# The beginning of a two-layer decoder trunk: loads in order of use, first products 512 columns wide, parameter loads later

## The chip, the core and the metric

The kernel runs on one core of one Trainium2 chip. The metric is the time of one execution in microseconds (us). The engines are called as in the profile: PE (TensorE), DVE (VectorE), ACT (ScalarE), POOL (GpSimd) and SP (SyncE, which here only starts DMAs). Each works through its own instructions in order and waits on semaphores for the others.

## What is computed

A trunk of two layers on x of 256 tokens by 1024 features, all float32. Each layer is a half-weighted SwiGLU block, a token mixer (gated linear attention, "gla", in layer 0; gated DeltaNet, "gdn", in layer 1) and a second SwiGLU block, each with an RMSNorm ahead and a residual sum behind, and a last RMSNorm.

```python
for i in range(DEPTH):                                   # DEPTH = 2
    x = x + 0.5 * swiglu(rmsnorm(x, norm_w[i, 0]), ffn_w_in[i, 0], ffn_w_out[i, 0])
    h = rmsnorm(x, norm_w[i, 1])
    x = x + (gla_mixer(h, ...) if i == 0 else gdn_mixer(h, ...))
    x = x + 0.5 * swiglu(rmsnorm(x, norm_w[i, 2]), ffn_w_in[i, 1], ffn_w_out[i, 1])
return rmsnorm(x, final_norm_w)

def swiglu(h, w_in, w_out):                              # w_in 1024 x 5632, w_out 2816 x 1024
    g, u = jnp.split(h @ w_in, 2, axis=-1)
    return (jax.nn.silu(g) * u) @ w_out
```

## The kernel before, in words

The stages are f00, gla, f01, f10, gdn, f11 (f: a SwiGLU block, class `FeedForward`). The 256 tokens are two blocks t = 0 and 1 of 128; x is transposed by PE to `xT` (`turn_x`, L307: four transposes of 128 by 128 for block t and feature half g, then four scaled copies to `xT`'s high part by ACT, and `lower`, four DVE operations that give the low part). Every product runs as three matmuls of a reduced float32 form: high by high, high by low and low by high.

**Weights.** Class `Weights` (L28) loads each weight block as a raw tile by SP (`_load`, four tiles in rotation) and cuts it into *parts* of 128 by 1024 numbers. A part is made in two steps: `high` has ACT cast the raw numbers (L69, "hi"), and `low` has DVE subtract the cast from the raw numbers (L76, "lo"). `take` hands the next part to PE. `high(n, held)` casts up to n further parts, but only while the number cast so far is below `taken - held + LOOK`, with LOOK = 7. In the stages' hand-ordered stretches `low` and `high` stand at fixed places between PE's work, so a part's cast and subtraction happen at the place where the count reaches it. In the `run` of a `FeedForward` stage `advance` refills to seven ahead after each take, and the instructions are ordered by a planner; everywhere else the order is as written.

**The start of a stage.** `step_over` (L1385) ends one stage and begins the next. It begins the next stage's first products (`units(0)`: block t = 0; `second_half` then ends them and runs `units(1)`: block 1), and calls `high(2, 4)` when a quarter has been issued twice:

```python
        low()
        high(2, 4)          # L1410, L1411
        second_half(st, fill)
```

For gla and gdn the first products are those of `first_columns` (L382), 512 columns wide; it takes all four parts at its first step (`parts.extend(W.take() for _ in range(4))`, L388). For a `FeedForward` they are those of `part` (L434), gate and up columns apart, 256 columns wide, and a part is taken when it is reached: two of four parts at the place of `high(2, 4)`.

**Behind it.** In gla's `run` (L704) the second value columns (`token_columns`, parts 5 to 8 of the stage) are followed by key and query columns (`load`: part 9 first). In gdn's `run` twelve pairs of `load` parts follow; `step(i)` (L1229) issues PE's products of pair i, parts 5 + 2i and 6 + 2i of the stage, in the pieces `fill(n[0])` to `fill(n[3])`; `fill(n[0])` is followed on DVE by the evacuation of pair i - 1 and two `low` calls, later in the step come the convolution's operations on DVE and two calls of `high(2)`, together two casts.

**The beginning of the program.** SP loads x in three pieces with the first two raw tiles between them (L213 to L217), POOL loads six small parameter tensors at once (`load_parameters`), PE warms up with `busy` products on constants, `turn_x` for block 0 and both halves comes first, then the first product part, then `turn_x` for block 1 between the parts. `parameters` (an Exp, a PE transpose, an ACT copy) stands in the middle of it.

Of the kernel before, what the change touches and what calls it, by code (L numbers as in the profile page):

```python
# [11 lines left out]
AF = mybir.ActivationFunctionType  # L12
# [15 lines left out]
class Weights:  # L28
# [79 lines left out]
def trunk(ctx: ExitStack, tc: tile.TileContext, x_in, norm_w, ffn_w_in, ffn_w_out, gla_w_in, gla_w_gk, gla_b_gk,  # L108
# [198 lines left out]
    def turn_x(N, t, g):  # L307
# [7 lines left out]
        for k in range(4):  # L315
            nc.scalar.activation(his[k], ps[:, k, :], AF.Copy, scale=ws[k])
# [65 lines left out]
    def first_columns(N, name, pss):  # L382

        parts = []

        def units(t):
            if t == 0:
                parts.extend(W.take() for _ in range(4))  # L388
            pss[t] = gup(f"tm_{name}{t}")[:, 0, :]
            for s in range(4):  # L390
                for k in range(2):
                    xh, xl = (N.xT[:, 2 * s + k, u + t * P:u + (t + 1) * P] for u in (0, 256))
                    hi, lo = parts[s]
                    nc.tensor.matmul(pss[t], lhsT=xh, rhs=hi[:, k, :], start=(s + k == 0), stop=False)
                    nc.tensor.matmul(pss[t], lhsT=xh, rhs=lo[:, k, :], start=False, stop=False)
                    nc.tensor.matmul(pss[t], lhsT=xl, rhs=hi[:, k, :], start=False, stop=(s == 3 and k == 1))
                    yield
                if t == 1:
                    low()
                    high(1, 3 - s)  # L400

        return units
# [25 lines left out]
    class FeedForward:  # L428
        factor, quarter, mids = 0.5, 4, {}

        def __init__(self, N):
            self.N, self.parts, self.ps, self.am, self.aTs = N, [], {}, [], {}

        def part(self, t, s, c):  # L434

            N, i = self.N, 2 * s + c
            while len(self.parts) <= i:
                self.parts.append(W.take())
            if t not in self.ps:
                self.ps[t] = gup(f"g0_{N.name}{t}")  # L440
            hi, lo = self.parts[i]
            for k in range(4):
                o = self.ps[t][:, c, 0:256]
                xh, xl = (N.xT[:, 4 * s + k, u + t * P:u + (t + 1) * P] for u in (0, 256))
                nc.tensor.matmul(o, lhsT=xh, rhs=hi[:, k, :], start=(s + k == 0), stop=False)  # L445
                nc.tensor.matmul(o, lhsT=xh, rhs=lo[:, k, :], start=False, stop=False)  # L446
                nc.tensor.matmul(o, lhsT=xl, rhs=hi[:, k, :], start=False, stop=(s == 1 and k == 3))  # L447
                yield

        def units(self, t):  # L450
            for s in range(2):
                for c in range(2):
                    yield from self.part(t, s, c)
                    if t == 1:
                        low()
                        high(1, 3 - 2 * s - c)

        def first(self, t):
            N, ps = self.N, self.ps[t]
            sl = small(f"sl0_{N.name}{t}", 256, tag="t1")  # L460
            nc.scalar.activation(sl, ps[:, 0, 0:256], AF.Silu, scale=N.r[t][:, 0:1])
            a = small(f"a0_{N.name}{t}", 256, tag="t1")
            nc.vector.scalar_tensor_tensor(a, ps[:, 1, 0:256], N.r[t][:, 0:1], sl, op0=ALU.mult, op1=ALU.mult)
# [131 lines left out]
    def gla(N):  # L595
# [22 lines left out]
        def gates():  # L618
            rows_bc(N)
            hold["z"] = narrow(N, "z")  # L620

# [4 lines left out]
        st.units = first_columns(N, "v0", ps0)  # L626
# [205 lines left out]
    def gdn(N):  # L832
# [63 lines left out]
        st.units = first_columns(N, "dr0", ps0)  # L896
# [562 lines left out]
    load_parameters()  # L1459
    N, st = make(stages[0])  # L1460
    with manual():
        constants()
        for g in range(2):
            lower = turn_x(N, 0, g)
# [3 lines left out]
        busy(8)  # L1468
        if isinstance(st, FeedForward):
            part = lambda *a: [None for _ in st.part(*a)]  # L1470
            part(0, 0, 0)
            for g in range(2):
                turn_x(N, 1, g)()
                high(1)
                low()
            part(0, 0, 1)
            parameters()
            rms(N, 0)
            for c in range(2):
                part(1, 0, c)  # L1480
            rms(N, 1)
            high(1)
            low()
            for t in range(2):
                for c in range(2):
                    part(t, 1, c)
# [3 lines left out]
        else:  # L1490
            turn_x(N, 1, 0)()
            turn_x(N, 1, 1)()
# [3 lines left out]
            parameters()  # L1496
# [43 lines left out]
```

## Time and profile before

| | us |
|---|---|
| three runs, median (lowest, highest) | 1045.27 (1044.95, 1045.68) |
| the profiled execution | 1045.1 |
| its span, first to last instruction | 1043.4 |
| PE busy in the span | 1027.3 |
| DVE busy | 701.0 |
| ACT busy | 590.4 |

The rows of the trace are in a section below. A row of the timeline gives the start, the busy time, the engine, the line, the operation, the output and the inputs, their sizes, how many instructions are merged in it and, in brackets, how long the engine sat idle before it and what ended that. Consecutive matmuls overlap, so the pace of PE is read from start to start, not from the busy time of one. A few records of PE can be missing from a trace or be given to a neighbouring line.

### The profile page before, as it was taken

Reading aid. Unit: us, or ns where it says so; the run is one execution under the profiler, and the core shown is the slowest. Engines: PE = TensorE matmul, PEld = TensorE weight load, DVE = VectorE, ACT = ScalarE, POOL = GpSimd, SP = SyncE. Lnnn points to the kernel's source line nnn. Section 1 sums busy time; section 2 is a strip of 40 time slices with the busy share of each in tenths; the row PEclk is TensorE's granted clock in tenths of the full one; section 3 lists DMA queues with packets and bytes.
Section 4 is the critical chain, followed back from the end, with each engine's and each line's share of the span. In section 5 each row is a group of like instructions: output and inputs, shape, how many; then the busy total and the mean of one; then the engine's idle time right before and its main releaser. Section 6 shows DMA issues by size and latency. Waiting matters only on the chain.

```text
span 1043.4 us, 15585 instructions
## 1 busy us (share of the span) xinstructions
PE 1027.3 (98%) x6162; PEld 892.0 (85%) x6162; DVE 701.0 (67%) x956; ACT 590.4 (57%) x1019; POOL 212.6 (20%) x250
## 2 busy tenths in 40 slices
PE   8999999999999999999999999999999999999996
PEld 8888888789889888888988888879989898888885
DVE  5866666666577666666766666578998776666664
ACT  7655555573556555555655555478677565555552
POOL 2111111103201111110111111117734401111111
PEclk9999999999999999999999999999999999999999
DMA  8764645444364564744564655544443156556431
GB/s 295 242 235 139 231 158 172 155 130 158 141 222 162 202 212 152 240 139 148 210 233 155 209 175 188 164 125 135 144 135 131 47 198 240 191 173 216 147 122 41
DMA packets 132410, 180.26 MB, mean 173 GB/s; under 512 B 5212, under 2 KB 111760, under 8 KB 132336
## 3 DMA queue, kind: packets, MB, share of 16 engines
q1 hardware_dynamic: 131712, 178.14, 51.0%
q0 software_dynamic: 416, 0.84, 0.4%
q8 instruction: 48, 0.79, 0.3%
q10 hardware_dynamic: 208, 0.29, 0.1%
q14 instruction: 26, 0.21, 0.1%
HBM read 178.20 MB, written 1.05 MB: 172 GB/s over the span
## 4 chain that ended last, share of the span: by engine, by line
PE 91%; DVE 3%; POOL 2%; issue 1%; DMA 1%; ACT 1%; SPq 0%; POOLq 0%; DVEq 0%; ACTq 0%
PE ps_f L341 29%; PE ps_f L342 15%; PE acc_f L414 7%; PE acc_f L413 7%; PE acc_f L415 7%; PE ps_d L576 2%; PE g_f L445 1%; PE g_f L447 1%; PE g_f L446 1%; PE ps_d L578 1%; PE ps_d L577 1%; DMA x<-in_x_dram 1%; POOL Mc L1002 1%; DVE lo L76 1%; PE acc_gdn L415 1%
## 5 line engine op out<-in xcount | busy, mean ns | idle before, releaser
L76 DVE TENSOR_TENSOR lo<-raw,hi 128x1024 fp32r<-128x1024 f32 x336 | 431.4, 1297 | 198.8 <-ACT hi L69 198.7
L69 ACT CAST hi<-raw 128x1024 fp32r<-128x1024 f32 x338 | 348.1, 1046 | 190.6 <-PE acc_f L415 83.7
L341 PE MATMUL ps_f<-xT_f,hi 128*128 128x512 f32 x1280 | 455.6, 398 | 0.0
L342 PE MATMUL ps_f<-xT_f,lo 128*128 128x256 f32 x1280 | 359.1, 281 | 0.0
L341 PEld LDWEIGHTS ps_f<-xT_f,hi 128*128 128x128 f32 x1280 | 240.5, 188 | 58.4
L342 PEld LDWEIGHTS ps_f<-xT_f,lo 128*128 128x128 f32 x1280 | 241.7, 189 | 2.8
L371 POOL TENSOR_TENSOR pair_f<-plo_f,Rb_f 128x512 f32<-128x512 f32 x76 | 102.8, 1352 | 558.6 <-DVE plo_f L369 558.6
L413 PE MATMUL acc_f<-hi,aT_f 128*128 128x512 f32 x352 | 138.4, 393 | 0.0
L414 PE MATMUL acc_f<-lo,aT_f 128*128 128x512 f32 x352 | 137.9, 392 | 0.0
L415 PE MATMUL acc_f<-hi,aT_f 128*128 128x512 f32 x352 | 137.0, 389 | 0.0
L413 PEld LDWEIGHTS acc_f<-hi,aT_f 128*128 128x128 f32 x352 | 66.1, 188 | 15.1
L415 PEld LDWEIGHTS acc_f<-hi,aT_f 128*128 128x128 f32 x352 | 66.1, 188 | 14.4
L414 PEld LDWEIGHTS acc_f<-lo,aT_f 128*128 128x128 f32 x352 | 66.1, 188 | 10.7
L405 ACT CAST aT_f<-a_f 128x256 fp32r<-128x256 f32 x80 | 32.5, 407 | 71.6 <-DVE a_f L483 71.4
L481 ACT ACTIVATE sl_f<-pair_f 128x256 f32<-128x256 f32 x80 | 33.5, 418 | 54.6 <-POOL pair_f L371 48.6
L369 DVE TENSOR_TENSOR plo_f<-ps_f,plo_f 128x512 f32<-128x512 f32 x80 | 54.7, 683 | 12.6 <-ACT plo_f L368 12.5
L406 DVE TENSOR_TENSOR aT_f<-a_f,aT_f 128x256 fp32r<-128x256 f32 x80 | 34.0, 425 | 36.0 <-ACT aT_f L405 36.0
L576 PE MATMUL ps_d<-xT_gdn,hi 128*128 128x256 f32 x192 | 56.5, 294 | 0.1
L578 PE MATMUL ps_d<-xT_gdn,lo 128*128 128x256 f32 x192 | 54.4, 283 | 1.1 <-DVE lo L76 1.1
L577 PE MATMUL ps_d<-xT_gdn,hi 128*128 128x256 f32 x192 | 54.2, 282 | 0.0
L368 ACT COPY plo_f<-ps_f 128x512 f32<-128x512 f32 x80 | 46.4, 580 | 12.8 <-PE ps_f L342 12.8
L483 DVE TENSOR_TENSOR a_f<-sl_f,pair_f 128x256 f32<-128x256 f32 x80 | 33.0, 413 | 10.4 <-ACT sl_f L481 10.4
(363 smaller groups left out, 1299.0 us busy)
## 6 DMA issues: line engine op xcount, KB each, us to landing
raw<-in_ffn_w_in_dram SPq DMA_DIRECT2D x80, 1024.0 KB, 5.4
raw<-in_ffn_w_out_dram SPq DMA_DIRECT2D x44, 1024.0 KB, 5.4
raw<-in_gdn_w_in_dram SPq DMA_DIRECT2D x16, 1024.0 KB, 5.4
raw<-in_gla_w_in_dram SPq DMA_DIRECT2D x12, 1024.0 KB, 5.1
raw<-in_ffn_w_in_dram SPq DMA_DIRECT2D x16, 512.0 KB, 3.5
raw<-in_gla_w_out_dram SPq DMA_DIRECT2D x4, 1024.0 KB, 5.0
raw<-in_gdn_w_out_dram SPq DMA_DIRECT2D x4, 1024.0 KB, 5.0
out_dram<-fin SPq DMA_DIRECT2D x3, 256.0 KB, 2.1
```

The costliest lines, as they stand in the source:

```text
L69: nc.scalar.copy(hv, src)
L76: self.nc.vector.tensor_tensor(lv, src, hv.bitcast(F32), op=ALU.subtract)
L341: nc.tensor.matmul(ps, lhsT=hi[:, k, :], rhs=N.xT[:, k, :], start=(k == 0), stop=False)
L342: nc.tensor.matmul(ps[:, 0:256], lhsT=lo[:, k, :], rhs=N.xT[:, k, 0:256], start=False, stop=(k == KT - 1))
L369: nc.vector.tensor_tensor(t, ps[:, :, 0:256], t, op=ALU.add)
L371: (eng or nc.gpsimd).tensor_tensor(dst, t, N.Rb.unsqueeze(1).broadcast_to([P, 2, 256]), op=ALU.mult)
L413: nc.tensor.matmul(accs[t][n], lhsT=ah, rhs=hi[:, 0, c], start=first, stop=False)
L414: nc.tensor.matmul(accs[t][n], lhsT=ah, rhs=lo[:, 0, c], start=False, stop=False)
L415: nc.tensor.matmul(accs[t][n], lhsT=al, rhs=hi[:, 0, c], start=False, stop=last)
L576: nc.tensor.matmul(o, lhsT=hi[:, k, :], rhs=xh, start=(k == 0), stop=False)
L577: nc.tensor.matmul(o, lhsT=hi[:, k, :], rhs=xl, start=False, stop=False)
L578: nc.tensor.matmul(o, lhsT=lo[:, k, :], rhs=xh, start=False, stop=(k == KT - 1))
```

## The change

What it does, piece by piece:

- Each `FeedForward`'s first weights come as four raw tiles of 256 rows with gate and up columns side by side (512 wide), each loaded by two DMAs of 256 KB, where there were four tiles of 512 rows with 256 columns and one DMA of 512 KB each.
- `FeedForward` uses `first_columns` for its first products: 24 matmuls of 512 columns for a block of tokens, in place of 48 of 256. Both blocks write one two-bank PSUM tile.
- `first_columns` takes a part when it reaches it, for all stages; its generator yields after three matmuls, twice a part.
- At the program's start SP issues x block 0 first half, raw tile 0, x block 1 first half, raw tile 1, then x's other halves, raw tiles 2 and 3. PE's order is: transposes of block 0 half 0, `busy`, products of block 0 with part 0, transposes of block 1 half 0, products of block 1 with part 0, transposes of the other halves, products with parts 1, 2 and 3 for both blocks. The first four scaled copies go to DVE. A one-element Silu stands on ACT ahead of the first cast.
- `load_parameters` moves behind the second block's norm, `parameters` into gla's `gates`.

```diff
@@ Weights._load
-            self.nc.sync.dma_start(tv, src)
+            if len(src.shape) == 3:
+                self.nc.sync.dma_start(tv, src)
+            else:
+                for a in range(shape[0]):
+                    self.nc.sync.dma_start(tv[:, a, :].rearrange("p (c f) -> p c f", c=src.shape[2]), src[:, a])
@@ trunk
-            for i in range(2):
-                for c in (0, FF):
-                    sub_rows(blk(w1, i * 512, 512, c, 256), 0, 4, 256)
+            for i in range(4):
+                w4 = w1[i * 256:(i + 1) * 256, :].rearrange("(k p) (c f) -> p k c f", p=P, c=2)
+                sub_rows(W.add_raw(w4[:, :, :, 0:256], (2, 512)), 0, 2, 512)
...
-    nc.sync.dma_start(x[:, 0, 512:1024], xv[:, 0, 512:1024])
+    W._load(0)
+    nc.sync.dma_start(x[:, 1, 0:512], xv[:, 1, 0:512])
     W._load(1)
-    nc.sync.dma_start(x[:, 1, :], xv[:, 1, :])
+    for t in range(2):
+        nc.sync.dma_start(x[:, t, 512:1024], xv[:, t, 512:1024])
+    W._load(3)
@@ turn_x(N, t, g, on_vector=False)
+            if on_vector:
+                nc.vector.tensor_scalar_mul(his[k], ps[:, k, :], ws[k])
+            else:
+                nc.scalar.activation(his[k], ps[:, k, :], AF.Copy, scale=ws[k])
@@ first_columns
+        def part(t, s):
+            while len(parts) <= s:
+                parts.append(W.take())
+            if not pss:
+                both = gup(f"tm_{name}")
+                pss.update({0: both[:, 0, :], 1: both[:, 1, :]})
+            hi, lo = parts[s]
+            for i, (u, w, k) in enumerate((u, w, k) for u, w in ((0, hi), (256, hi), (0, lo)) for k in range(2)):
+                nc.tensor.matmul(pss[t], lhsT=N.xT[:, 2 * s + k, u + t * P:u + (t + 1) * P], rhs=w[:, k, :],
+                                 start=(s + i == 0), stop=(s == 3 and i == 5))
+                if i % 3 == 2:
+                    yield
         def units(t):
-            if t == 0:
-                parts.extend(W.take() for _ in range(4))
-            pss[t] = gup(f"tm_{name}{t}")[:, 0, :]
             for s in range(4):
-                for k in range(2):
-                    ...
+                yield from part(t, s)
                 if t == 1:
                     low()
                     high(1, 3 - s)
@@ FeedForward
-        factor, quarter, mids = 0.5, 4, {}
+        factor, quarter, mids = 0.5, 2, {}
+            self.part, self.units = first_columns(N, f"g0_{N.name}", self.pss)
@@ gla: gates
             hold["z"] = narrow(N, "z")
+            parameters()
@@ the start
-    load_parameters()
     N, st = make(stages[0])
...
+            nc.scalar.activation(small("silu", 1), half, AF.Silu)
+            lower = turn_x(N, 0, 0, True)
             high(1)
             lower()
             low()
+            busy(8)
+            part(0, 0)
+            lower = turn_x(N, 1, 0)
+            high(1)
+            lower()
+            low()
+            part(1, 0)
+            lowers = [turn_x(N, t, 1) for t in range(2)]
+            high(1)
+            for lower in lowers:
+                lower()
+            for t in range(2):
+                part(t, 1)
+            low()
             rms(N, 0)
             high(1)
             low()
             for t in range(2):
+                part(t, 2)
+            rms(N, 1)
+            load_parameters()
+            for t in range(2):
+                part(t, 3)
                 st.first(t)
                 high(1)
                 low()
```

## Rows read from the trace of the kernel before

**Rows 1.** The page: its span, and the busy time and share of each engine.
```profile
span 1043.4 us, 15585 instructions
...
PE 1027.3 (98%) x6162; PEld 892.0 (85%) x6162; DVE 701.0 (67%) x956; ACT 590.4 (57%) x1019; POOL 212.6 (20%) x250
```
**Rows 2.** Waits of PE over the whole span: who waited for whom, us in total, times, the longest.
```profile
PE ps_d L578 <- DVE lo L76: 1.1, 2, 0.6
PE g_f L445 <- ACT hi L69: 1.0, 1, 1.0
```
**Rows 3.** The timeline of the first 24 us.
```profile
1.53 2.50 PE L236 MATMUL busy<-ones,ident 128*128 128x128 f32 x10 [1.53 <-POOL ident masks.py:199]
...
4.24 1.89 PE L312 MATMUL xps_f<-ident,x 128*128 128x128 f32 x8
...
5.45 1.14 ACT L316 ACTIVATE xT_f<-xps_f,nwc 128x128 fp32r<-128x128 f32 x4 [0.91 <-PE xps_f L312]
...
7.85 1.04 ACT L69 CAST hi<-raw 128x1024 fp32r<-128x1024 f32 x1 [1.25 <-DMA raw<-in_ffn_w_in_dram]
...
8.93 1.22 DVE L76 TENSOR_TENSOR lo<-raw,hi 128x1024 fp32r<-128x1024 f32 x1 [1.17 <-ACT hi L69]
...
12.04 1.10 PE L312 MATMUL xps_f<-ident,x 128*128 128x128 f32 x8 [0.27 <-DMA x<-in_x_dram]
12.74 1.14 ACT L316 ACTIVATE xT_f<-xps_f,nwc 128x128 fp32r<-128x128 f32 x4 [1.86 <-PE xps_f L312]
...
13.91 1.12 DVE L320 SCALAR_TENSOR_TENSOR xT_f<-xps_f,nwc,xT_f 128x128 fp32r<-128x128 f32 x4 [1.60 <-ACT xT_f L316]
...
20.51 1.28 ACT L461 ACT_TABLE_LOAD   x1
21.81 0.47 ACT L461 ACTIVATE sl_f<-g_f,rstd_f 128x256 f32<-128x256 f32 x1
...
23.59 0.28 PE L342 MATMUL ps_f<-xT_f,lo 128*128 128x256 f32 x1
```
**Rows 4.** DMA at the start: two lines of the issues of the first 30 us (out, in, queue, count, KB each, median us from issue to landing), and two stretches of 1 us (busy us and instructions of PE, PE's weight loads, DVE, ACT and POOL, granted clock, DMA share, GB/s).
```profile
raw<-in_ffn_w_in_dram SPq DMA_DIRECT2D x4, 512.0 KB, 8.7
...
x<-in_x_dram SPq DMA_DIRECT2D x1, 512.0 KB, 9.3
...
9.00:10.00 1.00, 0.33 (x1) 0.13 (x1) 1.00 (x1) 1.00 (x5) 0.00 (x0) 1.00 1.06 166
...
12.00:13.00 1.00, 0.96 (x9) 0.96 (x10) 0.32 (x1) 0.26 (x1) 0.00 (x0) 1.00 1.09 383
```
**Rows 5.** The pace of PE, from the timeline of PE: the first and the last of 36 matmuls of 256 columns in f00, and of 22 starts of 512 columns in gla.
```profile
18.83 0.28 PE L445 MATMUL g_f<-hi,xT_f 128*128 128x256 f32 x1
...
23.03 0.28 PE L447 MATMUL g_f<-hi,xT_f 128*128 128x256 f32 x1
...
207.96 0.40 PE L394 MATMUL tm_v<-hi,xT_gla 128*128 128x512 f32 x1
...
212.73 0.39 PE L589 MATMUL tm_v<-hi,xT_gla 128*128 128x512 f32 x1
```
**Rows 6.** The timeline of ACT in three step-overs, the casts at the place of `high(2, 4)`: into gla (the first of the two is a narrow part of 128 by 128), into f10 and into gdn (narrow first again).
```profile
202.74 1.26 ACT L69 CAST hi<-raw 128x128 fp32r<-128x128 f32 x2
...
500.51 1.07 ACT L69 CAST hi<-raw 128x1024 fp32r<-128x1024 f32 x1
...
687.43 1.26 ACT L69 CAST hi<-raw 128x128 fp32r<-128x128 f32 x2
```
**Rows 7.** gla: ACT's casts behind the gates' copies, DVE's subtractions, and the first product on PE that reads the low half of part 9, in order of time.
```profile
208.48 3.89 ACT L69 CAST hi<-raw 128x1024 fp32r<-128x1024 f32 x4
...
220.75 1.21 DVE L76 TENSOR_TENSOR lo<-raw,hi 128x1024 fp32r<-128x1024 f32 x1
...
226.00 0.28 PE L578 MATMUL ps_gk<-xT_gla,lo 128*128 128x256 f32 x1
...
227.46 2.35 DVE L76 TENSOR_TENSOR lo<-raw,hi 128x1024 fp32r<-128x1024 f32 x2
```
**Rows 8.** gdn, steps 6, 7 and 9: the first product of PE that reads the low half of a pair's second part (746.49 in step 6, 765.86 in step 9), DVE's two subtractions in the step, and PE's waits in between.
```profile
746.49 0.28 PE L578 MATMUL ps_d<-xT_gdn,lo 128*128 128x256 f32 x1
...
749.23 2.41 DVE L76 TENSOR_TENSOR lo<-raw,hi 128x1024 fp32r<-128x1024 f32 x2
...
750.51 0.38 PE L578 MATMUL ps_d<-xT_gdn,lo 128*128 128x256 f32 x1 [0.65 <-DVE lo L76]
...
765.86 0.28 PE L578 MATMUL ps_d<-xT_gdn,lo 128*128 128x256 f32 x1
...
770.10 2.03 PE L1048 MATMUL Y<-Mc,U 64*64 64x32 f32 x62 [0.78 <-ACT U L1036]
...
771.75 2.35 DVE L76 TENSOR_TENSOR lo<-raw,hi 128x1024 fp32r<-128x1024 f32 x2
...
773.01 0.39 PE L578 MATMUL ps_d<-xT_gdn,lo 128*128 128x256 f32 x1 [0.45 <-DVE lo L76]
```
**Rows 9.** The end of the program: PE's last matmul, and two stretches behind it (columns as in rows 4; the granted clock is the number ahead of the last two).
```profile
1034.51 0.39 PE L415 MATMUL acc_f<-hi,aT_f 128*128 128x512 f32 x1
...
1038.00:1040.00 2.00, 0.00 (x0) 0.00 (x0) 1.01 (x2) 0.72 (x1) 0.92 (x1) 1.00 0.14 54
1040.00:1042.00 2.00, 0.00 (x0) 0.00 (x0) 0.00 (x0) 0.00 (x0) 0.00 (x0) 0.54 0.68 262
```

More of the change, by code (lines that the diff above doesn't have):

```diff
@@ L305, in enter, with turn_x @@
         return N
-    def turn_x(N, t, g):
+    def turn_x(N, t, g, on_vector=False):
         ps = acc4(f"xps_{N.name}{t}{g}")
@@ L315, in turn_x @@
         for k in range(4):
-            nc.scalar.activation(his[k], ps[:, k, :], AF.Copy, scale=ws[k])
+            if on_vector:
+                nc.vector.tensor_scalar_mul(his[k], ps[:, k, :], ws[k])
+            else:
+                nc.scalar.activation(his[k], ps[:, k, :], AF.Copy, scale=ws[k])
         def lower():
@@ L384, in first_columns @@
         parts = []
+        def part(t, s):
[10 more added lines that the diff above has]
+                    yield
         def units(t):
-            if t == 0:
-                parts.extend(W.take() for _ in range(4))
-            pss[t] = gup(f"tm_{name}{t}")[:, 0, :]
             for s in range(4):
-                for k in range(2):
[L392 to L397, printed above, removed]
+                yield from part(t, s)
                 if t == 1:
@@ L400, in units @@
                     high(1, 3 - s)
-        return units
+        return part, units
     def split(dst_hi, dst_lo, src):
@@ L428, in trunk @@
     class FeedForward:
-        factor, quarter, mids = 0.5, 4, {}
+        factor, quarter, mids = 0.5, 2, {}
         def __init__(self, N):
[L432 to L456, printed above, removed]
+            self.N, self.pss, self.am, self.aTs = N, {}, [], {}
+            self.part, self.units = first_columns(N, f"g0_{N.name}", self.pss)
         def first(self, t):
-            N, ps = self.N, self.ps[t]
+            N, ps = self.N, self.pss[t]
             sl = small(f"sl0_{N.name}{t}", 256, tag="t1")
-            nc.scalar.activation(sl, ps[:, 0, 0:256], AF.Silu, scale=N.r[t][:, 0:1])
+            nc.scalar.activation(sl, ps[:, 0:256], AF.Silu, scale=N.r[t][:, 0:1])
             a = small(f"a0_{N.name}{t}", 256, tag="t1")
-            nc.vector.scalar_tensor_tensor(a, ps[:, 1, 0:256], N.r[t][:, 0:1], sl, op0=ALU.mult, op1=ALU.mult)
+            nc.vector.scalar_tensor_tensor(a, ps[:, 256:512], N.r[t][:, 0:1], sl, op0=ALU.mult, op1=ALU.mult)
             self.am.append(a)
@@ L625, in gla @@
         ps0 = {}
-        st.units = first_columns(N, "v0", ps0)
+        _, st.units = first_columns(N, "v0", ps0)
         st.first = lambda t: v_evac(ps0[t], t, 0)
@@ L895, in gdn @@
         ps0, ev0 = {}, gate_evac(N, srn, 0, 4, nwb[:, 256:384])
-        st.units = first_columns(N, "dr0", ps0)
+        _, st.units = first_columns(N, "dr0", ps0)
         st.first = lambda t: hold.update({"finish": ev0(ps0[t], t, t == 1)})
@@ L1462, in trunk @@
         constants()
-        for g in range(2):
-            lower = turn_x(N, 0, g)
+        if isinstance(st, FeedForward):
+            part = lambda *a: [None for _ in st.part(*a)]
+            nc.scalar.activation(small("silu", 1), half, AF.Silu)
+            lower = turn_x(N, 0, 0, True)
             high(1)
@@ L1467, in trunk @@
             low()
[L1468 to L1477, printed above, removed]
+            busy(8)
[12 more added lines that the diff above has]
+            low()
             rms(N, 0)
-            for c in range(2):
-                part(1, 0, c)
-            rms(N, 1)
             high(1)
@@ L1484, in trunk @@
             for t in range(2):
-                for c in range(2):
-                    part(t, 1, c)
+                part(t, 2)
[3 more added lines that the diff above has]
+                part(t, 3)
                 st.first(t)
@@ L1490, in trunk @@
         else:
-            turn_x(N, 1, 0)()
-            turn_x(N, 1, 1)()
+            for t in range(2):
+                for g in range(2):
+                    turn_x(N, t, g)()
             rms(N, 0)
@@ L1495, in trunk @@
             W.prefill()
-            parameters()
+            load_parameters()
             fill = filler(st.units(0))
```

## The prediction

> **What bounds the kernel now.** I read the page first: PE is busy 1027.3 of 1043.4 us [rows 1], so time is won or lost only where PE starts earlier, does less, or is made to wait. The waits of PE come next: they are few, and the largest behind the start is for low halves of weights in gdn, 1.1 us in two waits [rows 2]. Weights are ready only just in time there; a reader should keep that. Then I read the timeline of the start, where PE's stream becomes dense only at 12.04, when the last piece of x lands [rows 3], and the places in gla and gdn where the change alters the order in which weights are made ready [rows 6 to 8]. The sum is made against the profiled execution, 1045.1 us for a span of 1043.4; it lies 0.2 below the median of 1045.27.
>
> **Part 1, width of the products.** 256 columns go at (23.03 - 18.83) / 35 = 0.120 us, 512 columns at (212.73 - 207.96) / 21 = 0.227 [rows 5]. A FeedForward stage has 96 of the one before and 48 of the other after: 11.52 against 10.90, 0.6 us less. In f01, f10 and f11 these products are dense, so the 0.6 counts in full; transposes between them cost the same either way. Three stages: -1.7 (I take 0.57 each, since starts right behind transposes are a little slower). f00's share is in part 2.
>
> **Part 2, the start.** Loads: before, the 512 KB tiles took 8.7 us to land (median) and x's second block 9.3 [rows 4], part of it beside POOL's parameter loads, when the rate fell to 166 GB/s against 383 two us later [rows 4]. Raw tile 0 had landed at 7.85, when its cast started [rows 3]; it is now second in the queue, without those loads. I bound it by 5.4 and 7.8 and take 6.0, an estimate: 768 KB at some 300 GB/s, the middle of these rates, behind a first 2 us, plus one for the slowest engine. Extra DMA issues stand on SP only, which waits for buffers anyway.
>
> Now the chain, with durations from [rows 3]. Four transposes start at 4.24 and end at 5.4, as before. DVE makes the four high copies (not shown on DVE; bounds 0.8 and 1.4 around L320's 1.1, the nearest row, which I take) and the four low ones (1.1): 7.55. ACT loads Silu's table behind the copy of the norm weights (1.28) and runs the small Silu: 6.0, then the cast: 7.05. Low half of part 0: 7.55 + 1.2 = 8.7. PE, in order, cannot pass the two products that read it (0.5): 9.2. The next transposes stand behind them: 9.7. ACT's four copies: 10.85; DVE starts low copies only when all four are done, as at 12.74 and 13.91. Two low copies and the four products left: 12.3. The eight transposes, whose first four feed ACT after 0.6; eight copies on ACT: 15.1; the last four low copies behind them on DVE: 16.25; low half of part 2: 17.4. From there PE is dense: 14 products, 3.2, with their tail 20.8. But then Silu of block 0 (0.47) stands ahead of the cast of part 4 (1.04), and that ahead of its low half (1.22): 23.6. The first product of the main loop that reads it ran at 23.59 before. So PE is through with its first products near 22.2, some 0.9 earlier than before, and waits the gain away: **0.0**, with -0.8 (quick copies on DVE, half the coupling) and +1.5 (raw tile 0 at 7.8, which goes through the chain almost one to one) as ends. The moved parameter loads cost nothing: POOL issues them behind the second norm, and its next work was idle-waiting; the weights they run beside are needed some 12 us later.
>
> **Part 3, what the lazy take does to the look-ahead.** This is the term that decides. At `high(2, 4)` the stage's parts 0 to 3 have been cast. gla and gdn had taken four parts there, so the limit was 4 - 4 + 7 = 7 and two casts went out; f10 had taken two, limit 5, one cast. The rows show just this: two, one, two [rows 6]. After the change `first_columns` has taken two at that place, since a quarter of two yields, issued twice, is two parts. So gla and gdn cast one, and each later part takes the place of its successor, until some call meets its limit. In gla that is the first `high(2, 2)`, behind `k_evac(0, pk[0])`, in gdn the end of step 12. In the steps of gdn the old count sits at the limit exactly, so nothing catches up.
>
> Price in gla: part 9's low half moves from DVE's place at 220.75 to that at 227.46, behind the scan and the difference there, and is ready at 227.46 + 1.2 = 228.7. PE reads it at 226.00 [rows 7]. PE waits **2.7**; it has nothing else queued, and it is dense behind, so nothing gives that back. Bounds 1.5 and 3.5.
>
> Price in gdn: in each step the second part's low half now comes from the first `low` of the same step instead of the step before. In steps 1 to 5 it still arrives within 0.1 us of its product. In step 6 DVE is late with the solve's gathering: 749.23 + 1.2 = 750.45, read at 746.49 [rows 8]: 4.0. PE's old wait up to 750.51, 0.7 with the pace taken off, goes: net 3.3. DVE meanwhile works on things already ready, so its places don't shift. In step 9 the low half is ready at 771.75 + 1.2 = 772.95, behind the solve's back substitution; PE would read it at 765.86 + 3.3 = 769.2: 3.8. The waits of 0.78 and 0.45 behind it [rows 8], some 1.8 with weight loads and a short one that follows, fall away: net 2.0. Sum **5.3**, bounds 3 (DVE drawn earlier by what PE no longer contends for) and 9 (its places shift with PE by half).
>
> **Part 4, `parameters` in gla.** The transpose moves and costs the same. On ACT, Exp behind Silu needs a table load that wasn't there: L461's took 1.28 and the activation started 1.30 after it [rows 3]. Queued behind it are the casts from 208.48 [rows 7]: 208.5 + 1.3 + two short ones 0.4 + 1.05 = 211.2, low half 212.5; token columns read it 0.23 behind 212.73 [rows 5]. Zero, with 0.4 to spare; +0.1 for small things. The Trainium skill, "ScalarE: Activation LUTs", section "What ACT_TABLE_LOAD costs", gives about 2.66 us for a switch, a drain included, and so speaks against moving an Exp between Silu and Ln. The row shows half of that; by the page PE would wait, which is rival 4.
>
> **Sum.** -1.7 + 0.0 + 2.7 + 5.3 + 0.1 = +6.4: 1045.1 + 6.4 = 1051.5.
>
> **The rivals.**
> 1. Look-ahead costs nothing (the other side). If more than one cast goes out at `high(2, 4)` in gla, or the low halves reach DVE before its long operations, the 8.0 vanish: 1045.1 - 1.7 + 0.1 = 1043.5. Against it: [rows 6] show the count obeyed, and [rows 2] that there was no slack. It decides at whether part 9's low half ends before 226.0.
> 2. The clock falls in the new waits. The trace shows ten busy matmuls in 2.50 us at the start and eight transposes in 1.89 [rows 3], half the later pace, 1.2 against 2.4 GHz, from 1.53 to 6.13. If each of the two waits of about 4 us in gdn were followed by such a stretch of 4.6 us at half pace, each would cost 2.3 more: 1056.1. Against it: after the last matmul at 1034.51 the granted clock was still 1.00 in 1038 to 1040 and fell behind 1040 [rows 9]. The Trainium skill, "TensorE: Matmul & The Clock Gate", section "HAM oscillation", warns that a matmul stream broken by waits is throttled again; this trace has a wait of that length without it.
> 3. The start slips: raw tile 0 no sooner than 7.8: +1.5, 1053.0. For it: four loads share the queue from the first. Against it: x and POOL's loads leave its way.
> 4. The table load of part 4 with its drain holds ACT longer than its row: with a drain as long as the load itself, 1.3 more, less the 0.4 to spare, PE waits 0.9 for the token columns: 1052.4. (That is the page's rule of part 4; by its figure the wait is 1.0.) Against it: the activation began 1.30 behind the load's start [rows 3].
> 5. DVE's places shift in full with PE's waits, so that later second parts wait too. If the seven steps from 6 to 12 each paid half of what steps 6 and 9 pay on average (5.3 / 2), that is 9 more: 1060.5. Against it: DVE is without idle in that stretch.
>
> **How the numbers follow.** Forecast 0.60, rival 1 0.13, rival 2 0.07, rival 3 0.10, rival 4 0.05, rival 5 0.05. The range 1047.5 to 1056.5 holds the forecast with its bounds and rivals 2 to 4, and leaves out rivals 1 and 5 and a little of the forecast's tails, 0.2. This kernel's measurement can tell 0.2% (2.1 us) from no change: faster is below 1043.2, slower above 1047.4. Rival 1 lies on the edge of faster: 0.05 faster, 0.13 same with a good startup added to a cheap look-ahead, 0.82 slower.
>
> **What would show it.** Right: one cast between the last copy of x and the first evacuation in gla and gdn; a wait of PE for a low half of 2.7 near gla's first key product, of about 4 in gdn's steps 6 and 9; the first column products ending earlier but the main loop of f00 starting at the same time, behind a wait for a low half of about 1 us; 512-column products at 0.227. Wrong: no new waits on L76 (rival 1), a granted clock below 1.00 after them (rival 2), PE's first product later than 8 (rival 3). What would make it wrong altogether is a slack in DVE's order that I read as none.

## The result: 1059.55 us, 14 slower, outside the range

| | us |
|---|---|
| before, median of 4 | 1045.47 |
| changed kernel, median of 4 (lowest, highest) | 1059.55 (1058.57, 1060.69) |
| ratio, 95% interval | 1.0135 (1.0117 to 1.0152) |
| forecast (range) | 1051.5 (1047.5 to 1056.5) |

The direction was right; the size was not: 14 us where 6.4 were forecast. The profiled execution took 1058.57 with a span of 1056.9, so the spans differ by 13.5. The first lines of the page answer to [rows 1]:

```profile
span 1056.9 us, 15270 instructions
...
PE 1031.0 (98%) x5970; PEld 884.4 (84%) x5970; DVE 703.7 (67%) x960; ACT 591.2 (56%) x1017; POOL 210.3 (20%) x250
```

PE has 192 instructions fewer, as the wider products should give, and yet its busy time rose by 4 us: something runs slower, or several matmuls stand longer. The place of the loss comes from the starts of the stages. The first transpose of x marks each; the timeline of PE shows it in the kernel before

```profile
194.93 0.27 PE L312 MATMUL xps_gla<-ident,x 128*128 128x128 f32 x1
305.49 0.27 PE L312 MATMUL xps_f<-ident,x 128*128 128x128 f32 x1
492.59 0.27 PE L312 MATMUL xps_f<-ident,x 128*128 128x128 f32 x1
679.60 0.27 PE L312 MATMUL xps_gdn<-ident,x 128*128 128x128 f32 x1
845.69 0.27 PE L312 MATMUL xps_f<-ident,x 128*128 128x128 f32 x1
```

and in the changed one:

```profile
195.81 0.27 PE L321 MATMUL xps_gla<-ident,x 128*128 128x128 f32 x1
309.62 0.27 PE L321 MATMUL xps_f<-ident,x 128*128 128x128 f32 x1
496.99 0.27 PE L321 MATMUL xps_f<-ident,x 128*128 128x128 f32 x1
684.33 0.27 PE L321 MATMUL xps_gdn<-ident,x 128*128 128x128 f32 x1
858.77 0.27 PE L321 MATMUL xps_f<-ident,x 128*128 128x128 f32 x1
```

The differences of neighbouring starts are the lengths of the stages. Against the kernel before, in us (the last column runs to the end of the span; the experiments' rows come from their own traces in the same way):

| kernel | f00 | gla | f01 | f10 | gdn | f11, end | span |
|---|---|---|---|---|---|---|---|
| forecast | 0.0 | +2.8 | -0.6 | -0.6 | +5.3 | -0.6 | |
| changed kernel | +0.9 | +3.2 | +0.3 | +0.3 | +8.4 | +0.4 | 1056.9 |
| e1, a tile for each block | +0.7 | +2.0 | -0.7 | -0.6 | +5.9 | -0.6 | 1050.1 |
| e2, four parts taken | +0.9 | +0.1 | +0.3 | +0.4 | -0.1 | +0.4 | 1045.4 |
| e3, both | +0.6 | +0.1 | -0.7 | -0.5 | -0.1 | -0.6 | 1042.1 |
| e4, filled waits, gdn | +1.0 | +4.4 | +0.3 | +0.4 | +6.0 | +0.4 | 1055.9 |
| e10, filled waits, all | +0.9 | +3.2 | +0.2 | +0.3 | +5.5 | +0.4 | 1053.9 |
| e7, e3 with halves | +1.0 | +0.2 | 0.0 | 0.0 | 0.0 | -0.1 | 1044.4 |
| e8, e3, start of before | +2.4 | 0.0 | -0.7 | -0.6 | -0.1 | -0.5 | 1043.8 |
| e5, e3, new order of start | -2.4 | +0.1 | -0.7 | -0.6 | -0.1 | -0.6 | 1039.1 |
| e11, e5, parameters early | +4.0 | 0.0 | -0.7 | -0.6 | -0.1 | -0.6 | 1045.4 |
| e12, e5, copies on ACT | -0.9 | +0.1 | -0.7 | -0.6 | 0.0 | -0.6 | 1040.6 |
| e6, e5, later gates | -2.5 | -0.5 | -0.7 | -0.5 | +0.4 | -0.6 | 1038.9 |
| e9, e5, later gates in gla | -2.9 | -0.5 | -0.7 | -0.6 | -0.1 | -0.6 | 1037.9 |

Every stage is longer than forecast. The largest terms, in gla and gdn, stand where the look-ahead was expected; the waits of PE, to be held beside [rows 2], say what else is there:

```profile
PE ps_d L574 <- DVE lo L81: 7.1, 2, 3.6
PE ps_gk L574 <- DVE lo L81: 2.6, 1, 2.6
PE ps_f L354 <- DVE lo L81: 2.0, 3, 0.7
...
PE tm_g_f L408 <- DVE a_f L459: 1.1, 1, 1.1
PE tm_v L408 <- ACT v L620: 0.8, 1, 0.8
PE tm_dr L408 <- ACT gdn_srn L544: 0.8, 1, 0.8
```

The first two lines are the forecast ones. The last three are new in kind: first products (tm_) that wait for the evacuation (a_f, v, gdn_srn) of the *other* block.

**The look-ahead, as forecast.** At the place of `high(2, 4)` in gla and gdn ACT has one narrow cast, where [rows 6] have two (timeline of ACT):

```profile
203.62 0.31 ACT L74 CAST hi<-raw 128x128 fp32r<-128x128 f32 x1
...
692.14 0.31 ACT L74 CAST hi<-raw 128x128 fp32r<-128x128 f32 x1
```

Low halves and the products that wait for them, from the timelines of DVE and PE in gla, step 6 and step 9 of gdn; they answer to [rows 7, 8]:

```profile
228.76 2.35 DVE L81 TENSOR_TENSOR lo<-raw,hi 128x1024 fp32r<-128x1024 f32 x2
...
754.26 2.41 DVE L81 TENSOR_TENSOR lo<-raw,hi 128x1024 fp32r<-128x1024 f32 x2
...
778.38 2.35 DVE L81 TENSOR_TENSOR lo<-raw,hi 128x1024 fp32r<-128x1024 f32 x2
```
```profile
230.03 0.39 PE L574 MATMUL ps_gk<-xT_gla,lo 128*128 128x256 f32 x1 [2.63 <-DVE lo L81]
...
755.55 0.58 PE L574 MATMUL ps_d<-xT_gdn,lo 128*128 128x256 f32 x1 [3.64 <-DVE lo L81]
755.93 0.41 PE L572 MATMUL ps_d<-xT_gdn,hi 128*128 128x256 f32 x1
...
760.78 0.28 PE L574 MATMUL ps_d<-xT_gdn,lo 128*128 128x256 f32 x1
...
779.65 0.39 PE L574 MATMUL ps_d<-xT_gdn,lo 128*128 128x256 f32 x1 [3.47 <-DVE lo L81]
```

Each product starts some 0.1 us behind the end of the first of DVE's two subtractions: the part's low half was made one place too late, at the three places that the prediction named.

**What was not expected behind them.** From 755.55 to 760.78 PE takes 5.23 us for the products that took 750.51 - 746.49 = 4.02 before, a wait of 0.65 among it [rows 8]: 1.9 us lost with PE never idle. The products start every 0.21 us (755.93 to the next ones) where 0.120 is the pace of [rows 5]. The stretches with the granted clock (columns as in [rows 4]) say why:

```profile
229.00:232.00 3.00, 1.97 (x16) 1.97 (x17) 2.11 (x2) 3.00 (x5) 0.00 (x0) 1.00 0.00 0
...
756.00:761.00 5.00, 5.00 (x26) 5.00 (x26) 3.48 (x8) 2.88 (x5) 4.14 (x12) 0.53 0.68 213
761.00:766.00 5.00, 5.00 (x45) 5.00 (x43) 5.00 (x9) 0.91 (x2) 4.45 (x8) 1.00 0.41 109
...
779.60:784.00 4.40, 4.35 (x26) 4.35 (x26) 1.93 (x3) 1.98 (x6) 0.00 (x0) 0.68 0.70 213
```

The granted clock is 0.53 behind the first wait in gdn and 1.00 again from 761, and 0.68 in the stretch behind the second; behind gla's shorter wait it stayed 1.00 in this execution. A busy PE with 26 matmuls in 5 us beside one with 45 is how half the clock (1.2 in place of 2.4 GHz) looks in a profile, and why PE's busy time rose.

**What was not expected in the FeedForward stages.** Timeline of f00's start (ACT, DVE and PE), block one's Silu, its product and block two's first products:

```profile
21.54 0.47 ACT L457 ACTIVATE sl_f<-tm_g_f,rstd_f 128x256 f32<-128x256 f32 x1 [1.58 <-PE tm_g_f L408]
...
22.04 0.48 DVE L459 SCALAR_TENSOR_TENSOR a_f<-tm_g_f,rstd_f,sl_f 128x256 f32<-128x256 f32 x1 [1.84 <-ACT sl_f L457]
...
22.58 1.20 PE L408 MATMUL tm_g_f<-hi,xT_f 128*128 128x512 f32 x4 [1.15 <-DVE a_f L459]
```

Block two writes its own bank, but of the tile that block one is read from, and it starts 0.06 us after that read. In f01, f10 and f11 the planner puts four products of the main loop into this gap, and the first low half that they need isn't there yet (timeline of f01):

```profile
318.96 0.39 PE L353 MATMUL ps_f<-xT_f,hi 128*128 128x512 f32 x1
...
319.89 0.48 DVE L459 SCALAR_TENSOR_TENSOR a_f<-tm_g_f,rstd_f,sl_f 128x256 f32<-128x256 f32 x1
320.02 0.39 PE L354 MATMUL ps_f<-xT_f,lo 128*128 128x256 f32 x1 [0.67 <-DVE lo L81]
...
320.60 1.09 PE L408 MATMUL tm_g_f<-hi,xT_f 128*128 128x512 f32 x4
```

So three theories stood to be told apart: the look-ahead alone; the tile that both blocks share; and the clock that falls in the waits.

### The profile page after: what moved, and what is told of

It is laid out like the page before. It is cut to its first block, busy times and chain, and to the rows that moved or that the text cites. A ratio compares the mean times of both kernels' runs of the same rounds, so it can differ in the third digit from the quotient of the medians.

```text
span 1056.9 us, 15270 instructions
## 1 busy us (share of the span) xinstructions
PE 1031.0 (98%) x5970; PEld 884.4 (84%) x5970; DVE 703.7 (67%) x960; ACT 591.2 (56%) x1017; POOL 210.3 (20%) x250
## 4 chain that ended last, share of the span: by engine, by line
PE 90%; DVE 4%; ACT 2%; POOL 2%; issue 2%; POOLq 0%; ACTq 0%; DVEq 0%
PE ps_f L353 28%; PE ps_f L354 14%; PE acc_f L431 7%; PE acc_f L432 7%; PE acc_f L433 7%; PE tm_g_f L408 3%; PE ps_d L572 2%; PE ps_d L574 1%; PE ps_d L573 1%; DVE lo L81 1%; PE tm_dr L408 1%; PE tm_v L408 1%; POOL Mc L999 1%; PE acc_gdn L433 1%; PE acc_gla L433 1%
## 5 line engine op out<-in xcount | busy, mean ns | idle before, releaser
L572 PE MATMUL ps_d<-xT_gdn,hi 128*128 128x256 f32 x192 | 58.0, 302 | 0.0
L573 PE MATMUL ps_d<-xT_gdn,hi 128*128 128x256 f32 x192 | 55.8, 291 | 0.0
L574 PEld LDWEIGHTS ps_d<-xT_gdn,lo 128*128 128x128 f32 x192 | 38.4, 200 | 7.6 <-DVE lo L81 7.5
```

The costliest lines, as they stand in the source:

```text
L572: nc.tensor.matmul(o, lhsT=hi[:, k, :], rhs=xh, start=(k == 0), stop=False)
L573: nc.tensor.matmul(o, lhsT=hi[:, k, :], rhs=xl, start=False, stop=False)
L574: nc.tensor.matmul(o, lhsT=lo[:, k, :], rhs=xh, start=False, stop=(k == KT - 1))
```

## The experiments

**e1_two_tiles.** The changed kernel with

```diff
-            if not pss:
-                both = gup(f"tm_{name}")
-                pss.update({0: both[:, 0, :], 1: both[:, 1, :]})
+            if t not in pss:
+                pss[t] = gup(f"tm_{name}{t}")[:, 0, :]
```

> The changed kernel, with a PSUM tile of its own for each block of the first products. Theory A: the tile that both blocks share makes block two's first product wait until block one's result has been read out. The changed kernel waits 1.1 us for that in f00, 0.8 in gla and 0.8 in gdn, and 0.7 for a low half in each of f01, f10 and f11, where products of the main loop were put in between. Those six waits go. Some of it comes back, because PE waited 0.7 in gla and in gdn for the second rstd before: three times 0.85, 0.4 in f00 and 0.2 in the mixers, together 3.2, so about 1056.3. The two long waits in gdn stay. Rival B: the order of PE doesn't matter there and the time lies with the look-ahead alone: 1059.5, no change.

Measured: 1054.73 (1051.84 to 1057.20), ratio 1.0088 (1.0064 to 1.0113), 4.8 below the changed kernel. The waits for evacuations are gone, and so are the three for ps_f's low half in f01, f10 and f11. A new one of 0.7 for a low half shows in f00, and those of the look-ahead stand:

```profile
PE ps_d L573 <- DVE lo L81: 7.1, 2, 3.6
PE ps_gk L573 <- DVE lo L81: 2.6, 1, 2.6
...
PE ps_f L354 <- DVE lo L81: 0.7, 1, 0.7
```

f01, f10 and f11 fall by 1.0 each, to 0.6 to 0.7 below the kernel before. Theory A holds. In gla 1.2 are won while the wait for the low half stays: 0.8 is the wait at tm_v, and the 0.7 for the second rstd, which the expectation had coming back, did not; where the other 0.4 lay is not shown. gdn's gain of 2.4 in the table is not the tile alone: its wait at tm_dr was 0.8, and in this execution the clock fell behind one of gdn's two long waits only (see the last section).

**e2_four_taken.** The changed kernel with, in `units`,

```diff
+            if t == 0 and N.name in ("gla", "gdn"):
+                parts.extend(W.take() for _ in range(4))
```

> The changed kernel, with gla and gdn taking all four first parts at the first step again, as before. Theory A: the lost look-ahead is the cause of the waits for low halves in gla (2.6 us) and gdn (7.1 in two), and the waits in gdn of about 3.5 us also halve PE's pace for a stretch behind each (1.9 and 1.4): both go, 2.8 + 8.3 less, about 1048.4. Rival B: PE's half pace has another cause than the waits, contention with the solve: 2.8 + 5.3 less, about 1051.5. Rival C: the waits come from DVE's later work, not from the count of casts: no change, 1059.5.

Measured: 1047.55 (1046.86 to 1048.15), ratio 1.0017 (1.0005 to 1.0028), 12.0 less than the changed kernel. gla and gdn are within 0.1 us of the kernel before; the others are as in the changed kernel. The lost look-ahead causes the long waits and, since the half pace goes with them, that too.

**e3_both.** Both edits.

> The changed kernel with both edits: a PSUM tile for each block, and four parts taken at once in gla and gdn. If the two costs are independent, 1059.5 - 3.2 - 11.1 = 1045.2, and the three FeedForward stages behind the first take 0.57 less than in the kernel before, the start decides the rest. If one hides behind the other (the wait at the shared tile gives weights time), it is between 1046 and 1048.

Measured: 1044.69 (1043.78 to 1046.41), ratio 0.9988 (0.9976 to 1.0), near the first case. Together they take 14.9, and 4.8 + 12.0 one by one: about 2 us of them overlap. By the profiles 1.2 of that are in gla, where the shared tile costs 1.2 with the look-ahead lost and nothing without (e2 against e3 in the table): PE waits 0.6 at tm_v in e2 and 0.7 for the second rstd, as in the kernel before, in e3. The rest can't be told from what the clock did in e1's runs. What is left of the change is -0.6 in each later FeedForward stage and +0.6 in f00.

**e4_busy_wait and e10_busy_all.** The changed kernel with, in `load`, ahead of the product that waits (`extra` gives 20 in gdn's pairs 6 and 9 in e4; 16 there and 12 at gla's first key product in e10, whose lines these are):

```diff
+                for _ in range(extra.get((s, k), 0)):
+                    nc.tensor.matmul(ps[:, 1 - s, 384:512], lhsT=ident, rhs=ones, start=True, stop=True)
                 nc.tensor.matmul(o, lhsT=lo[:, k, :], rhs=xh, start=False, stop=(k == KT - 1))
```

> The changed kernel with 20 more products of constants on PE, put just ahead of the product that waits for the low half in gdn's pairs 6 and 9, into columns of the pair's PSUM tile that nothing reads. They add no value to the result. Theory A: PE's idle time of 3.5 us makes the granted clock fall to half, which costs 1.9 and 1.4 us behind the waits. With PE at work in the waits the clock stays at 1.00 and the low halves come as late as before: 3.3 less, about 1056.2. Rival B: the half pace comes from something else (traffic, the solve beside it): no change, 1059.5, or more by what the added products take.

Measured: 1057.52 (1056.20 to 1057.85), 2.0 below the changed kernel where 3.3 were expected. The trace gives two reasons. The 20 products ran for some 4.5 us, longer than the wait, so that PE came late to the low half; and in gla, where nothing was filled, this execution had the clock fall in the wait of 2.6 that had cost no clock in the changed kernel's profile:

```profile
229.00:232.00 3.00, 1.85 (x8) 1.85 (x9) 2.23 (x2) 3.00 (x5) 0.00 (x0) 0.60 0.00 0
```

e10 was made to test this reading.

> The changed kernel with products of constants in all three waits for low halves, 16 in gdn's pairs 6 and 9 (3.6 us at the pace of e4) and 12 ahead of gla's first key product (2.7 us), into columns of the tile that nothing reads. Theory A: the waits stay as long as they are and only the clock is held: gdn 3.4 less than in the changed kernel, gla 0.6 (half of the times that it lost 1.2 there), together 1055.6, with less spread between executions. Rival B: the clock falls for another cause: 1059.5 with the spread of the changed kernel.

Measured: 1055.69 (1055.65 to 1055.71), ratio 1.0099 (1.0085 to 1.0113). The forecast was met, and the four runs lie within 0.06 us, where the changed kernel's lie within 2.1 and those of e1 within 5.4. The clock is 1.00 in the stretches that had 0.60 and 0.53:

```profile
229.00:232.00 3.00, 3.00 (x26) 2.86 (x25) 2.09 (x2) 3.00 (x5) 0.00 (x0) 1.00 0.00 0
...
756.00:761.00 5.00, 5.00 (x44) 5.00 (x43) 5.00 (x10) 3.62 (x7) 4.31 (x9) 1.00 0.71 210
```

gdn is 2.9 us shorter than in the changed kernel's profile. In step 6 DVE makes the low half when it did there (754.18 for 754.26); in step 9, which in the changed kernel lies behind the stretch at half pace, 1.4 sooner (timelines of PE and DVE):

```profile
773.58 0.28 PE L573 MATMUL ps_d<-xT_gdn,hi 128*128 128x256 f32 x1
773.70 3.74 PE L575 MATMUL ps_d<-ones,ident 128*128 128x128 f32 x32
...
776.93 2.35 DVE L81 TENSOR_TENSOR lo<-raw,hi 128x1024 fp32r<-128x1024 f32 x2
...
778.20 0.39 PE L576 MATMUL ps_d<-xT_gdn,lo 128*128 128x256 f32 x1 [0.76 <-DVE lo L81]
```

So of gdn's 8.4 the waits make 5.5 and the clock, with what it shifts on DVE, 2.9.

**e7_halves.** e3 with every first product of a FeedForward stage as two of 256 columns, in two banks:

```diff
+                for c in range(2) if N.name[0] == "f" else (None,):
+                    out, cols = (pss[t], slice(0, 512)) if c is None else (pss[t][:, c, 0:256], slice(256 * c, 256 * c + 256))
+                    nc.tensor.matmul(out, lhsT=N.xT[:, 2 * s + k, u + t * P:u + (t + 1) * P], rhs=w[:, k, cols],
...
```

> The kernel with both edits, and each first product of the FeedForward stages made as two of 256 columns, gate and up in a bank of their own. Theory A (the width is worth 0.57 us in a dense stage): f01, f10 and f11 0.57 longer each, f00 0.3 to 0.6: 2.1 more than 1044.7, about 1046.8. Rival B: the width is worth nothing because weight loads or waits set the pace: 1044.7.

Measured: 1046.31 (1045.72 to 1046.89), ratio 1.0002 (0.9993 to 1.001): 1.6 more than e3. f01 and f10 have the length of the kernel before to 0.01 us, so the 0.5 to 0.7 that e3 gains in each are the width. f00 loses 0.4, not its full share: it waits for other things.

**e8_old_start.** e3 with the beginning of the program as before (loads, order, copies on ACT, parameters early), and products still 512 wide. The edit takes back the diff's last block, its order of the loads of x and raw tiles, and the move of `parameters`; each raw tile still comes by two DMAs.

> The kernel with both edits, and the start in the order of before: x first, both halves of block one transposed before the first products, copies on ACT, parameter loads and parameters at the start, no early Silu; the products stay 512 wide. Theory A (the new order of the start gains nothing because the main loop waits for part 4): the main loop starts 0.6 to 0.9 earlier than in the kernel with both edits, 1044.0. Rival B: the new order is worth what its earlier first product shows, some 1 us: 1045.7.

Measured: 1045.26 (1043.19 to 1046.92), ratio 0.999 (0.998 to 0.9999), 0.6 above e3 (0.2 by the ratios to the kernel before, which was run beside each), with intervals that overlap: **inconclusive** between the theories. In the profiled execution PE waited 3.1 us for x's second block (0.3 in [rows 3]), and the granted clock was 0.72 from 12 to 16 us. The twelve runs spread over 3.7 us, more than the theories differ.

**e5_start_order.** e3 with the start in a third order:

```diff
-            part(0, 0)
-            lower = turn_x(N, 1, 0)
+            begun = st.part(0, 0)
+            next(begun)
+            lower = turn_x(N, 1, 0)
+            for _ in begun:
+                pass
             high(1)
             lower()
             low()
+            lowers = [turn_x(N, 0, 1)]
             part(1, 0)
-            lowers = [turn_x(N, t, 1) for t in range(2)]
+            lowers.append(turn_x(N, 1, 1))
...
             low()
+            high(1)
+            low()
             rms(N, 0)
-            high(1)
-            low()
...
             load_parameters()
+            high(1)
+            low()
             for t in range(2):
                 part(t, 3)
                 st.first(t)
-                high(1)
-                low()
+                if t == 0:
+                    high(1)
+                    low()
```

> The kernel with both edits, and the start put into another order: the transposes of block two's first half between the third and the fourth product of block one with part 0; the transposes of block one's second half ahead of block two's products with part 0; high and low half of part 3 ahead of the sums of squares, those of part 4 ahead of the Silu of block one. Theory A: in the start PE waits for the chain of transposes, copies and low halves (0.3 + 0.5 + 0.4 + 0.5 us in the kernel with both edits) and at the main loop 0.6 more for part 4's low half: some 2 us less, about 1042.7. Rival B: the main loop's weights or their loads set its start: no change from 1044.7.

Measured: 1041.75 (1040.49 to 1042.63), ratio 0.9958 (0.9944 to 0.9971), 2.9 below e3: theory A, a little more than expected. The main loop starts at 21.04, with the low half of part 4 ready before it is read, and f00 is 2.4 shorter than before. Which of its three moves gives how much was not tried.

**e11_early_params and e12_act_copies** put single parts of the change's start back into e5.

```diff
-            parameters()
...
+    load_parameters()
     N, st = make(stages[0])
...
+            parameters()
             rms(N, 0)
...
-            load_parameters()
```

> As e5_start_order, with the parameter loads and parameters at the start again (loads ahead of the first stage, the Exp between part 3 and the first sums of squares). Theory A: two more table loads of 1.28 us and some 0.5 us of work on ACT stand ahead of part 4's cast and of Silu, and POOL's loads beside x and the raw tiles: the main loop starts some 1 us later, gla gains 0.1: 1042.7. Rival B: ACT has the slack, since products of PE still run then: 1041.7.

Measured: 1046.85 (1045.42 to 1047.89), 5.1 above e5, and above theory A by 4. The table loads are not the first thing: PE waits for x (waits of PE, and the stretch from 4 to 8 us with DMA share and GB/s last; e5 has 0.7 us and 285 GB/s there).

```profile
PE xps_f L321 <- DMA x<-in_x_dram: 3.2, 1, 3.2
PE ps_f L353 <- DVE a_f L460: 1.8, 1, 1.8
```
```profile
4.00:8.00 4.00, 4.00 (x24) 3.85 (x24) 2.54 (x9) 2.73 (x4) 3.14 (x6) 1.00 0.70 213
8.00:12.00 4.00, 1.55 (x9) 0.99 (x7) 1.88 (x5) 1.14 (x4) 0.00 (x0) 1.00 0.98 307
12.00:16.00 4.00, 3.25 (x12) 2.59 (x13) 2.35 (x5) 2.19 (x5) 0.00 (x0) 0.66 1.07 374
```

Behind the wait for x the clock fell again (0.66). The wait for a_f is the chain of ACT, table loads included, which theory A had. Why x lands late is not shown: the kernel before, with the same parameter loads at its start, moved 291 GB/s from 4 to 8 us and waited 0.3 for x.

```diff
-            nc.scalar.activation(small("silu", 1), half, AF.Silu)
-            lower = turn_x(N, 0, 0, True)
+            lower = turn_x(N, 0, 0)
```

> As e5_start_order, with the first four copies of x on ACT and no early Silu. Theory A: the cast of part 0 stands behind four copies on ACT (0.4 later), and Silu's table load of 1.28 us comes ahead of the first Silu, behind part 4's cast: 0.4 more, 1042.2. Rival B: the table load delays part 5's cast and low half, which the main loop needs 2.8 us after its start: up to 1.7 more, 1043.4.

Measured: 1042.51 (1041.74 to 1044.22), 0.8 above e5 (1.4 by the ratios), between the two theories; the intervals of the ratios, 0.9962 to 0.998 and 0.9944 to 0.9971, overlap. PE waited 0.6 for part 0's cast and 0.8 for the a_f behind the table load.

**e6_start_gates and e9_gla_gates.** e5 with `st.mids = {2: gates, ...}` in place of `{1: gates, ...}`, in both mixers and in gla alone.

> As the run e5_start_order, and the transposes of rstd in gla and gdn stand three products later. Theory A: the two waits of 0.7 us for POOL's second rstd in gla and gdn go: 1.2 less than e5_start_order, about 1041.5. Rival B: the gates are late themselves and what they delay costs as much: no change from e5_start_order, or up to 1 us more.

> As e6_start_gates, with the later transposes of rstd in gla alone; in gdn they stand as before. Theory A: in e6 gla gained 0.7 and gdn lost 0.5 (stage lengths of the profiles), so this one keeps the gain alone: 0.5 less than e6, about 1039.7. Rival B: gdn's 0.5 in e6 was one execution's chance: the same as e6 or up to 0.7 more, 1040.2 to 1040.9.

Measured: 1040.18 (1039.37 to 1041.09), ratio 0.9943 (0.9931 to 0.9956), and 1040.62 (1040.19 to 1040.79), ratio 0.9954 (0.9942 to 0.9967). By the medians they lie 1.6 and 1.1 below e5, where theory A of e6 had 1.2; but the kernel before was 0.7 lower when it was run beside e9 than beside e5 and e6, by the ratios it is 1.6 and 0.4, and all three intervals overlap, so the gain is not clear of the noise. The two waits of 0.7 us for rstd are gone in e6, and gla's in e9. By the profiles gdn loses 0.5 in e6 and not in e9 (spans 1038.9 and 1037.9), but the runs don't bear that out: theory A of e9 fell, and which of the two is better stays open. Either beats both kernels: e6 is 0.57% faster than the one before.

## Why the prediction was wrong, step by step

Two terms that stood at nothing in the sum were each near 3 us: the clock behind gdn's waits (2.9) and the tile that both blocks share (2.7). Without either one of them the 1058.57 of the profiled execution would lie inside the range.

**Part 3, the look-ahead: right.** One cast in place of two, the three places, and the waits: PE's idle time was 2.6, 3.6 and 3.5 us where 2.7, 4.0 and 3.8 had been worked out. gdn's net 5.3 measured 5.5 with the clock held (e10), and e2 removes it all. That 3.5 lies so near 3.8 is partly luck: half pace behind the first wait brought both PE and DVE later to step 9. With the clock held, PE goes 4.3 us there without a product of weights (773.86 to 778.20). Rival 1 is out, and rival 5 too: PE waits for low halves in gdn only twice, DVE's place in step 6 moved by 754.26 - 749.23 = 5.03, 0.3 more than gdn's start (684.33 - 679.60), and that in step 9, with the clock held, by 776.93 - 771.75 = 5.18. So PE's wait in step 6 didn't shift DVE; the half pace did (778.38 - 771.75 = 6.63 in the changed kernel).

**Rival 2, the clock, given 0.07: it happened, in gdn.** The step that failed is "this trace has a wait of that length without it": the end of the program, where no matmul followed, was taken as evidence for waits in which PE must go on. The rival's price of 4.6 for two waits was high; e10 measures 2.9 in gdn. The Trainium skill, "TensorE: Matmul & The Clock Gate", section "HAM oscillation", which warns that a matmul stream broken by waits is throttled again, was the better guide: the granted clock of 0.53 behind a wait agrees with it.

**Part 1, the width: right in size, wrong in the sum.** 0.57 a stage was forecast; e3 gains 0.5 to 0.7 and e7 takes it back. But the stages became 0.3 to 0.4 *longer*, because the change's line that gives both blocks one tile was described and never priced: "In f01, f10 and f11 these products are dense, so the 0.6 counts in full" doesn't ask what block two's first product now waits for. e1 shows it: 1.0 in each of three stages, 2.9 in the medians between e2 and e3. This was the largest missing term together with the clock.

**Part 2, the start: right in shape, 0.9 too early.** The main loop did wait away what the first products gained: Silu of block one came at 21.54 where 20.8 had been worked out. The tile's wait of 1.15 covered part 4's low half here, so that removing it brings 0.3 only (e2 against e3) and 0.6 of waiting for the low half shows in its place. The other 0.6 of f00 is in the chain ahead: ACT began the copies of block two's first half at 10.17, where 9.7 had been worked out, and the low half of part 2 was still 0.5 late, at 17.91 for 17.4 (timeline of the changed kernel):

```profile
10.17 1.14 ACT L328 ACTIVATE xT_f<-xps_f,nwc 128x128 fp32r<-128x128 f32 x4 [2.57 <-PE xps_f L321]
...
16.70 1.21 DVE L81 TENSOR_TENSOR lo<-raw,hi 128x1024 fp32r<-128x1024 f32 x1
```

"The moved parameter loads cost nothing" was tested by no run for the place where they went; e11, which puts loads and `parameters` back together in an order of start that needs x early, is 5.1 longer. Rival 3 didn't come: raw tile 0's cast started at 6.55 and the first product at 7.65.

**Part 4: small, as taken.** gla's +0.1 in e2 and e3, with the table load in place, leaves no room for rival 4, and with `parameters` back at the start (e8, e11) gla is at 0.0.

The account in the spans, against the forecast sum of 6.4: the tile in three stages 2.7 (+1.0 where -1.7 stood), the clock 2.9, f00 0.9, gla 0.4 (the tile again, by e1), gdn's waits 0.2; together 7.1, and 6.4 + 7.1 = 13.5.

## What to carry to other kernels

Where operations are issued by a count (taken parts, buffers held), a change to *when* the count moves shifts everything behind it: list each call that reads the count and what it finds there. When two results are given one tile, ask what the second one's first write now waits for, even if the banks differ. And price a wait of the matmul engine in the middle of a stream as the wait and a stretch at half pace behind it, at a chance, unless something can keep the engine at work.

## What the runs showed of the hardware

- The clock falls in some waits and not in others of the same length. gla's wait of 2.6 us left it at 1.00 in the changed kernel and at 0.60 in e4; behind gdn's second wait of some 3.5 us it was 0.68 in the changed kernel and 1.00 in e1:

```profile
776.00:780.00 4.00, 4.00 (x70) 3.87 (x70) 1.25 (x3) 1.31 (x5) 0.00 (x0) 1.00 0.84 256
```

  This goes with the spread between executions: e1's six runs lie at 1051.84 to 1053.15 with a mean granted clock of 0.994 or 0.995 and at 1056.32 to 1057.20 with 0.989; e10's four, where products of constants fill the waits, lie within 0.06 us at 0.997 or 0.998. The kernel before, run beside e1, had one such run too, 1051.93 at 0.990, beside 22 from 1044.20 to 1046.79. What decides it within one kernel stays open.
- The parameter loads on POOL's queue take more of the DMA engines than their bytes say. In the first 12 us of e11 (DMA by queue: packets, MB, share of 16 engines) POOL's 0.30 MB take 13.6% of the engines' time, 45% for a MB, beside 25% for a MB on SP's queue; in e5, where only w_gk's are left, they take 1.9%:

```profile
q1 hardware_dynamic: 1906, 2.32, 57.7%
q0 software_dynamic: 259, 0.30, 13.6%
```

  The Trainium skill, "DMA: Bandwidth & Descriptors", section "Why small descriptors are slow (HBM only)", puts a fixed cost on each packet. That is not what makes these dear: in e11's trace the 165 packets of 4 bytes took 9 ns each, 1.5 us of the queue's 26 us of engine time, and the 48 of 4096 bytes, which together have the size of the two norm weights written to all partitions, took 398 ns each, 19 us, twice the time for a byte of SP's packets of 1024 bytes (50 ns each). Why they do is not shown, and neither is that these loads delay x by the 2.5 us that PE waits longer in e11.
